# Zero-padding the 64-row contractions to 128 rows, with one relative-position row per head and queries in reverse order

## The chip, the core and the metric

The kernel runs on one core of a Trainium2 chip. The core has a matrix engine (PE; its weight loads, PEld, are listed apart), a vector engine (DVE), a scalar engine (ACT), GpSimd (POOL), and queues that start DMA transfers (SP's, ACT's, POOL's). The metric is the device time of one execution in microseconds (us), as a median over runs; lower is better.

## What is computed

Two transformer-like blocks of width 1024 run one after the other over the same 512 tokens, in float32. The parts that the change touches are these, cut to the core:

```python
# block 1, sliding-window attention: 8 heads of 64, 2 key heads, window 128
s = einsum("bnqkgd,bnskd->bnkgqs", qb, kb) * 64 ** -0.5      # contraction over 64
logits = where(valid, s + rel_table[rel_bucket(rel)], NEG_INF)   # bias by distance only
# block 1, indexed attention (DSA): 8 heads of 64 over a latent of 128
q_lat = einsum("bthd,hcd->bthc", q, w_uk) * 64 ** -0.5       # contraction over 64
dots  = einsum("bqhd,bsd->bqhs", iq, ik) * 64 ** -0.5        # 8 indexer heads of 64
score = einsum("bqh,bqhs->bqs", iw, relu(dots)); idx = top_k(score, 128)
logits = einsum("bqhc,bqkc->bhqk", q_lat, c_kv[idx]) + rel_table[rel_bucket(t - idx)]
# block 2, MLA: 16 heads, scores over 128 (nope) + 64 (rope) dimensions
q_full, k_full = concat([q_nope, q_rope]), concat([k_nope, k_rope])
s = einsum("bqhd,bkhd->bhqk", q_full, k_full) * 192 ** -0.5
```

Around them stand dense products: input and output projections, a cross attention to 256 memory rows, a feed-forward of 4096, and a state-space mixer (SSM) in block 2.

## The kernel before

Every float32 product is made of three matmuls on halves: a tensor is split in a high part H and a rest L, and `mm3` (L126 to L130) adds H·H, L·H and H·L in one PSUM bank. Weights arrive on SP's queue as `wraw` (512 KB, from `win_s` and the like); ACT rounds them to `wh` (L120), POOL subtracts for `wl` (L123). The framework gives each engine one in-order stream; a scheduler fixes the order when the program is built, and releases of tiles and PSUM banks become waits.

The program goes through these stages, in us of the span: memory keys, layer norm and the first input projections (0 to 90); the indexer (90 to 137), where PE also makes the memory values (`mem_v`, tile `acc`); more input projections with the top-k rounds on DVE (to 172); sliding-window attention, `swa`, with three more projections as filler (to 237); the DSA heads (to 300); the output projection, cross attention and feed-forward; the SSM mixer; MLA's input projection (to 1457), MLA's 16 heads (1457 to 1685) and the output projection.

Where the contraction is 64 long, the matmul uses 64 of PE's 128 rows:

- Indexer, per head and block of 128 queries: L446 multiplies all 128 rows (H of the query in one half, L in the other, both against `ikT` H), L447 multiplies the 64 rows of the H half by `ikT` L. ACT takes the relu (`rl`, L449), DVE adds it up (`sc`, L451 and L453). `ev_iq` (L407) fills `iq`; the L half goes to the other rows by a DMA on SP's queue (L414).
- `swa` scores: `sc<-kaH,qaH` and its two fellows, on the half that belongs to the key head.
- DSA `proj(h)` (L487): `mm<-qbH,wh`, 64 rows.
- MLA `scores`: three matmuls of 128 rows for nope, one of 128 rows for the rope part (L1371), one of 64 rows (L1372), for each of 16 heads and 4 blocks.

The bias by distance comes from a row per head. `bias_rows` (L820) makes these rows and writes each of them 64 times to DRAM, in `usd` (8 x 64 x 384) and `udd` (8 x 64 x 640). `bias_tile` (L816) reads a tile in which each partition starts one element earlier than the one above it, in two transfers of 64 rows: `bA` for `swa`, `bB` (one buffer) for DSA.

`attn_pipeline` (L870) runs a head's projection two heads ahead. The pool `dsaq`, which holds `bB` and `ql`, is opened before `swa`, so the scheduler can place work of the first DSA heads in `swa`'s tail.

Of the kernel before, what the change touches and what calls it, by code (L numbers as in the profile page):

```python
# [7 lines left out]
F32 = mybir.dt.float32  # L8
# [4 lines left out]
P = 128  # L13
# [3 lines left out]
NEG = -1e30  # L17
BR = 64
ALPHA = 2.0 ** 0.25
# [6 lines left out]
class Net:  # L26
# [51 lines left out]
    def consts(self):  # L78
        nc = self.nc
        self.ident = self.load(self.cp, "ident", [P, P])  # L80
        self.identr = self.cp.tile([P, P], F32R, tag="identr", name="identr")
        nc.vector.tensor_copy(self.identr, self.ident)
        self.mhalf = self.cp.tile([P, 16], F32, tag="mhalf", name="mhalf")
        nc.vector.memset(self.mhalf, -0.5)
        self.eps = {}
        for e in (1e-5, 1e-6):
            self.eps[e] = self.cp.tile([P, 1], F32, tag=f"eps{e}", name=self.nm("eps"))
            nc.vector.memset(self.eps[e], 4 * e)
        t = self.cp.tile([P, 1], F32, name="root")
        nc.scalar.activation(t, self.eps[1e-5], AF.Sqrt)  # L90
# [198 lines left out]
    def block1(self, dbg):  # L289
# [46 lines left out]
        dp = ctx.enter_context(self.tc.tile_pool(name="dp", bufs=1, space=bass.MemoryType.DRAM))  # L336
        usd = dp.tile([8, BR, 384], F32, name="usd")
        udd = dp.tile([8, BR, 640], F32, name="udd")
        ap = ctx.enter_context(self.pool("attn"))
# [11 lines left out]
        sq = c2.enter_context(self.pool("selfq"))  # L351
        ka = self.pair(sq, [P, T], "ka")
        qa = self.pair(sq, [P, 4, T], "qa")
        ikT = self.pair(sq, [P, T], "ikT")
        c3 = ExitStack()
        ap = c3.enter_context(self.pool("small"))
# [19 lines left out]
        ssq = ap.tile([P, NT], F32, name="ssq")  # L376
        junk = ap.tile([P, P], F32, name="junk")
        for v in vp:
# [3 lines left out]
        for t in range(NT):  # L382
            nc.vector.tensor_tensor(ms[t], accs[t][:, :328], bm, op=ALU.add)
            m = ms[t]
            nc.vector.tensor_scalar_mul(iw[:, t, :], m[:, 320:328], 8.0 ** -0.5)
            nc.scalar.activation(junk, m[:, 128:256], AF.Square, accum_out=ssq[:, t:t + 1])
# [20 lines left out]
        def ev_iq(i, ps):  # L407
            L = self.mp.tile([P, T], F32R, tag="vo", name=self.nm("ql"), bufs=2)
            for x, lo in zip(iq, (0, 64)):
                b = slice(lo, lo + 64)  # L410
                nc.scalar.activation(x[b, i, :], ps[b], AF.Identity, bias=bs[b, i:i + 1])
                nc.vector.scalar_tensor_tensor(L[b], ps[b], bs[b, i:i + 1], f32(x[b, i, :]), op0=ALU.add, op1=ALU.subtract)
            for x, lo in zip(iq, (0, 64)):
                nc.sync.dma_start(f32(x[64 - lo:128 - lo, i, :]), f32(L[lo:lo + 64]))  # L414

        def ev(i, ps):
            if i < 4:
                return ev_iq(i, ps)
            H, L = [None, ka, (x[:, i - 5, :] for x in qa), (x[:, i - 9, :] for x in qb)][0 if i < 4 else 1 if i < 5 else 2 if i < 9 else 3]
            if 4 <= i < 9:  # L420
                F = self.mp.tile([P, T], F32, tag="vo", name=self.nm("qf"), bufs=2)
                self.split_g(H, L, ps, F, bs[:, i:i + 1])
# [5 lines left out]
        for src, dst in ((ikf, ikT), (cf, cT)):  # L428
# [3 lines left out]
            self.split(dst[0], dst[1], ps)  # L432
        self.split(cM[0], cM[1], cf)
# [4 lines left out]
        for n in range(1, NT):  # L438
# [3 lines left out]
            for h in range(8):  # L442
                half = slice((h % 2) * 64, (h % 2) * 64 + 64)
                ps = self.mm()
                x = iq[h % 2]
                nc.tensor.matmul(ps[:, :w], x[:, h // 2, q], ikT[0][:, :w], start=True, stop=False, skip_group_check=True)  # L446
                nc.tensor.matmul(ps[:, :w], x[half, h // 2, q], ikT[1][half, :w], start=False, stop=True, skip_group_check=True)  # L447
                rl = self.mp.tile([P, 512], F32, tag="vo", name=self.nm("rl"), bufs=2)
# [22 lines left out]
        self.banks(sc=2, tr=2, pv=1, uv=1, mm=2)  # L471
        c4 = ExitStack()
        dq = c4.enter_context(self.pool("dsaq", "right"))
        mixA = self.pair(pa, [P, 4, T], "iq")
        self.swa(c2, mixA, qa, ka, vp, snk, usd, lambda x: self.gemm_s([a["win_s"][9 + x]], xt, lambda i, ps: ev(x + 9, ps)))
        self.flush()
        c2.close()
        sp = ctx.enter_context(self.pool("dsa"))
        self.gemm_s([a["win_s"][12]], xt, lambda i, ps: ev(12, ps))
# [3 lines left out]

        ukH, ukL = self.wload(a["w_uk"], n=512)
        uvH, uvL = self.wload(a["w_uv"])
        st = {}

        def proj(h):
            half = slice((h % 2) * 64, (h % 2) * 64 + 64)
            uc = slice((h // 2) * P, (h // 2 + 1) * P)  # L490
            bt = dq.tile([P, 512], F32, tag="bB", name=self.nm("bB"), bufs=1)
            self.bias_tile(bt, udd, h, 640, 512)
            ps = self.mm()
            self.mm3(ps, ukH[half, uc], ukL[half, uc], qb[0][half, h // 2, :], qb[1][half, h // 2, :], True, True)
            ql = self.pair(dq, [P, T], "ql", bufs=2)
# [8 lines left out]
        def out(h, PT):  # L504
# [8 lines left out]
            if h % 2 == 1:  # L513
                self.split(mix[0][:, 4 + h // 2, :], mix[1][:, 4 + h // 2, :], st["o"])
        self.attn_pipeline(sp, 8, proj, scores, out)
# [60 lines left out]
    def mem_k(self, W, wk):  # L576
        nc, a, mp = self.nc, self.a, self.mp

        def evk(i, ps):
            o = mp.tile([P, 256], F32, tag="ko", name=self.nm("ko"), bufs=3)  # L580
            nc.scalar.activation(o, ps, AF.Identity, bias=self.kb[:, i:i + 1])
            nc.sync.dma_start(self.kd[:, i * 256:(i + 1) * 256], o)
# [162 lines left out]
    def swa(self, c2, mix, qa, ka, vp, snk, usd, fill):  # L745
# [6 lines left out]
        def scores(pr, kv):  # L752
            h = pr + 4 * kv
            half = slice(kv * 64, kv * 64 + 64)
            bt = sp.tile([P, 256], F32, tag="bA", name=self.nm("bA"), bufs=2)
            self.bias_tile(bt, usd, h, 384, 256)
            Ss = []
            for n0 in (0, 2):
# [5 lines left out]
                for i in range(2):  # L764
# [4 lines left out]
                    o = ps[:, i * 256 + lo:i * 256 + 256]  # L769
                    self.mm3(o, qa[0][half, pr, q], qa[1][half, pr, q], ka[0][half, ks], ka[1][half, ks], i == 0, True)  # L770
                for i in range(2):
# [14 lines left out]
        for x, (pr, kv) in enumerate(heads):  # L786
# [18 lines left out]
            if kv == 1:  # L805
                self.split(mix[0][:, pr, :], mix[1][:, pr, :], acco)
            if x % 2 == 0 and x < 6:
# [410 lines left out]
    def block2b(self, dbg):  # L1218
# [4 lines left out]
        ckv = self.pair(lp, [P, 2, T], "ckv")  # L1223
        kr = self.pair(lp, [P, T], "kr")
        cs = self.load(lp, "rope_cs", [P, NT, 32])
        sn = self.load(lp, "rope_sn", [P, NT, 32])
        dmask = self.load(lp, "dmask", [P, T])
        zd = self.dram.tile([P, 16, T], F32, name="zd")
        with self.pool("mlain") as ip, self.pool("mlaz", "right") as zp:
# [39 lines left out]
            def trk():  # L1269
# [94 lines left out]
        def scores(h, n):  # L1364
# [76 lines left out]
def host(inp):  # L1441
# [152 lines left out]
```

## Time and profile before

| | |
|---|---|
| median of 3 runs | 1775.38 us (1775.02 to 1777.21) |
| the profiled execution | 1775.11 us |
| its span, first to last instruction | 1772.9 us |
| outside the span | 2.2 us |
| mean granted clock of PE | 0.985 |
| busy share: PE, PEld, DVE, ACT, POOL | 96%, 83%, 52%, 47%, 51% |

The profile is of one execution. "Busy" counts the modelled duration of matmuls, which overlap in the pipeline, so a PE that is busy all the time need not run at its peak: the distance from one matmul's start to the next one's start tells how fast it goes. A wait is given with the instruction that ended it. The granted clock is 1.00 at the higher of PE's two levels (2.4 GHz) and 0.50 at the lower (1.2 GHz).

### The profile page before, as it was taken

What the parts mean: (1) busy time and instruction counts of PE and PEld (TensorE: products, weight loads), DVE (VectorE), ACT (ScalarE), POOL (GpSimd) and SP (SyncE); (2) the same over time, 40 slices, a digit from 0 to 9 for tenths busy, and PEclk for the clock granted to TensorE, in tenths of its full rate; (3) what the DMA queues carried; (4) which work ended last, traced back from release to release, by engine and by line L of the source; (5) the groups of instructions that cost most, each with busy time, mean ns of one, the idle gap of its engine ahead of it and who ended that gap; (6) DMA issues with size and microseconds to landing.
All of it is one profiled execution on the core that took longest, in us unless ns stands there. A gap on an engine that the chain in (4) does not pass through costs nothing.

```text
span 1772.9 us, 27243 instructions
## 1 busy us (share of the span) xinstructions
PE 1699.5 (96%) x10203; PEld 1478.9 (83%) x10203; DVE 923.4 (52%) x1981; ACT 835.1 (47%) x1692; POOL 901.4 (51%) x825
## 2 busy tenths in 40 slices
PE   6979999899999999999999899998999999999998
PEld 6857779898988888887878788888999888888898
DVE  7448864634653004403778877788130325656522
ACT  4434664443343124313557677766333435555532
POOL 5726432452465445544558778776444534334341
PEclk8989999999999999999999999999999999999999
DMA  7654221532232222222332222332344331112341
GB/s 286 191 102 142 73 72 43 187 123 72 72 131 95 95 95 96 91 92 94 128 115 101 76 95 99 108 107 78 143 135 134 132 107 63 60 49 91 106 137 48
DMA packets 69444, 189.02 MB, mean 107 GB/s; under 512 B 10224, under 2 KB 17304, under 8 KB 69056
## 3 DMA queue, kind: packets, MB, share of 16 engines
q1 hardware_dynamic: 50128, 152.69, 25.2%
q10 hardware_dynamic: 18896, 32.50, 6.4%
q0 software_dynamic: 288, 2.10, 0.3%
q8 instruction: 80, 1.31, 0.3%
q14 instruction: 52, 0.43, 0.1%
HBM read 163.59 MB, written 16.84 MB: 102 GB/s over the span
## 4 chain that ended last, share of the span: by engine, by line
PE 74%; DVE 11%; ACT 5%; DMA 5%; issue 3%; POOL 2%; ACTq 0%; DVEq 0%; SPq 0%; POOLq 0%
PE mm L128 13%; PE mm L130 12%; PE mm L129 12%; PE acc L129 5%; PE acc L128 5%; PE acc L130 5%; PE sc L128 3%; PE sc L129 2%; PE sc L130 2%; DMA Dm<-acd 2%; DVE xbc L923 2%; PE pv L129 2%; PE pv L128 2%; PE pv L130 2%; PE tr L862 1%
## 5 line engine op out<-in xcount | busy, mean ns | idle before, releaser
L123 POOL TENSOR_TENSOR wl<-wraw,wh 128x512 fp32r<-128x512 f32 (+3 forms) x497 | 662.9, 1357 | 537.3 <-ACT wh L120 521.8
L120 ACT ACTIVATE wh<-wraw 128x1024 fp32r<-128x1024 f32 (+5 forms) x254 | 257.9, 1017 | 427.2 <-PE acc L130 125.5
L128 PE MATMUL mm<-xaH,wh 128*128 128x512 f32 x552 | 222.1, 402 | 0.0
L130 PE MATMUL mm<-xaH,wl 128*128 128x512 f32 x552 | 221.8, 402 | 0.0
L129 PE MATMUL mm<-xaL,wh 128*128 128x512 f32 x552 | 221.2, 401 | 0.0
L128 PE MATMUL mm<-wh,xaH 128*128 128x256 f32 x512 | 145.2, 284 | 1.4 <-ACT xaH L144 1.4
L130 PE MATMUL mm<-wh,xaL 128*128 128x256 f32 x512 | 144.6, 284 | 0.9 <-DVE xaL L142 0.9
L129 PE MATMUL mm<-wl,xaH 128*128 128x256 f32 x512 | 144.0, 282 | 0.0
L130 PEld LDWEIGHTS mm<-xaH,wl 128*128 128x128 f32 x552 | 105.3, 191 | 24.8
L128 PEld LDWEIGHTS mm<-xaH,wh 128*128 128x128 f32 x552 | 105.4, 191 | 24.4 <-issue 0.4
L129 PEld LDWEIGHTS mm<-xaL,wh 128*128 128x128 f32 x552 | 105.4, 191 | 24.3
L853 POOL TENSOR_SCALAR S<-S,den 128x128 f32<-128x128 f32 (+1 forms) x96 | 50.9, 533 | 122.1 <-DVE den L852 111.6
L128 PEld LDWEIGHTS mm<-wh,xaH 128*128 128x128 f32 x512 | 96.5, 188 | 2.0 <-ACT xaH L144 1.8
L130 PE MATMUL mm<-wh,xbL 128*128 128x256 f32 x336 | 94.7, 285 | 2.4 <-DVE xbL L142 2.3
L130 PEld LDWEIGHTS mm<-wh,xaL 128*128 128x128 f32 x512 | 96.0, 188 | 1.1 <-DVE xaL L142 1.1
L129 PEld LDWEIGHTS mm<-wl,xaH 128*128 128x128 f32 x512 | 96.5, 189 | 0.2
L128 PE MATMUL mm<-wh,xbH 128*128 128x256 f32 x336 | 95.2, 284 | 0.7 <-DVE lnsum L255 0.5
L129 PE MATMUL mm<-wl,xbH 128*128 128x256 f32 x336 | 94.5, 282 | 0.0
L680 DVE TENSOR_TENSOR rl<-rl 128x512 f32<-128x512 f32 x32 | 42.3, 1321 | 80.3 <-ACT rl L679 80.3
L923 DVE SCALAR_TENSOR_TENSOR xbc<-mm,conv_w,xbc 128x511 f32<-128x511 f32 (+2 forms) x84 | 62.2, 742 | 18.4 <-ACT xbc L921 17.5
L130 PEld LDWEIGHTS mm<-wh,xbL 128*128 128x128 f32 x336 | 62.8, 188 | 3.5 <-DVE xbL L142 2.9
L851 ACT ACTIVATE S<-S,mx 128x128 f32<-128x128 f32 (+1 forms) x96 | 53.7, 560 | 23.6 <-DVE mx L850 21.9
(616 smaller groups left out, 4777.9 us busy)
## 6 DMA issues: line engine op xcount, KB each, us to landing
wraw<-in_w_up SPq DMA_DIRECT2D x32, 512.0 KB, 3.2
wraw<-in_w_down SPq DMA_DIRECT2D x32, 512.0 KB, 3.2
wraw<-in_ssm_xbc SPq DMA_DIRECT2D x32, 512.0 KB, 3.2
Dm<-acd ACTq DMA_DIRECT2D x32, 256.0 KB, 3.4
wraw<-in_ssm_out SPq DMA_DIRECT2D x16, 512.0 KB, 3.5
wraw<-in_mla_z SPq DMA_DIRECT2D x16, 512.0 KB, 3.5
wraw<-in_mla_out SPq DMA_DIRECT2D x16, 512.0 KB, 3.5
wraw<-in_ssm_z SPq DMA_DIRECT2D x14, 512.0 KB, 3.3
```

The lines of the kernel that those rows point to most:

```text
L120: nc.scalar.activation(h[:, :n], raw[:, :n], AF.Copy)
L123: (leng or nc.gpsimd).tensor_tensor(l[:, e], raw[:, e], f32(h[:, e]), op=ALU.subtract)
L128: mm(out, aH, bH, start=first, stop=False, skip_group_check=True)
L129: mm(out, aH, bL, start=False, stop=False, skip_group_check=True)
L130: mm(out, aL, bH, start=False, stop=last, skip_group_check=True)
L680: nc.vector.tensor_tensor(r, r, r, op=ALU.mult)
L851: nc.scalar.activation(s, s, AF.Exp, bias=mx, scale=-1.0, accum_out=den)
L853: nc.gpsimd.tensor_scalar(s, s, den, 1.0, op0=ALU.mult, op1=ALU.mult)
L862: self.nc.tensor.transpose(pt[:, c], S[:, c], self.ident)
L923: nc.vector.scalar_tensor_tensor(o[:, j:], ps[:, :T - j], cw[:, m, 3 - j:4 - j], o[:, j:], op0=ALU.mult, op1=ALU.add)
```

## The change

All contractions of 64 get 128 rows, of which 64 are zero. `ka` becomes two pairs of tiles, one for each key head, with the other half zeroed; `ikT` L gets zeros in its upper half and H of every indexer query now stands in the lower half; `w_uk` is padded in DRAM (512 KB in place of 256 KB); MLA's `kr` H gets zeros in its lower half. The zeros are written by GpSimd.

The rows of relative positions are written once per head. A read then starts one element later on each next partition, and so the queries of a block stand in reverse order; `rev` turns them round when PSUM is read into `qa`, `qb` and, after attention, into the mix, and the identity for the masks (`identr`) is reversed too. The pool `dsaq` is opened after `swa`'s pool is closed. Two scratch tiles move to other memory.

```diff
-        nc.vector.tensor_copy(self.identr, self.ident)
+        b = self.identr[:, P - 1:P]
+        nc.vector.tensor_copy(bass.AP(b.tensor, b.offset, [b.ap[0], [-1, P]]), self.ident)
...
-        usd = dp.tile([8, BR, 384], F32, name="usd")
-        udd = dp.tile([8, BR, 640], F32, name="udd")
+        usd = dp.tile([8, 384], F32, name="usd")
+        udd = dp.tile([8, 640], F32, name="udd")
...
-        ka = self.pair(sq, [P, T], "ka")
+        ka = [self.pair(sq, [P, T], f"ka{kv}") for kv in range(2)]
+        for kv in range(2):
+            o = slice(64 - kv * 64, 128 - kv * 64)
+            for x in ka[kv]:
+                nc.gpsimd.memset(f32(x[o, :]), 0.0)
...
+        nc.gpsimd.memset(f32(ikT[1][64:, :]), 0.0)
...
+            if i == 4:
+                F = self.mp.tile([P, T], F32, tag="vo", name=self.nm("kf"), bufs=2)
+                for kv in range(2):
+                    b = slice(kv * 64, kv * 64 + 64)
+                    self.split_g(ka[kv][0][b, :], ka[kv][1][b, :], ps[b], F[b, :], bs[b, i:i + 1])
+                return
+            H, L = (self.blocks(x[:, i - 5, :] if i < 9 else x[:, i - 9, :]) for x in (qa if i < 9 else qb))
+            ps = self.rev(ps)
...
-                nc.tensor.matmul(ps[:, :w], x[half, h // 2, q], ikT[1][half, :w], start=False, stop=True, skip_group_check=True)
+                nc.tensor.matmul(ps[:, :w], x[:, h // 2, q], ikT[1][:, :w], start=False, stop=True, skip_group_check=True)
...
-        c4 = ExitStack()
-        dq = c4.enter_context(self.pool("dsaq", "right"))
         mixA = self.pair(pa, [P, 4, T], "iq")
         self.swa(c2, mixA, qa, ka, vp, snk, usd, lambda x: self.gemm_s([a["win_s"][9 + x]], xt, lambda i, ps: ev(x + 9, ps)))
         self.flush()
         c2.close()
+        c4 = ExitStack()
+        dq = c4.enter_context(self.pool("dsaq", "right"))
...
-            self.mm3(ps, ukH[half, uc], ukL[half, uc], qb[0][half, h // 2, :], qb[1][half, h // 2, :], True, True)
+            self.mm3(ps, ukH[:, uc], ukL[:, uc], qb[0][:, h // 2, :], qb[1][:, h // 2, :], True, True)
...
-                    self.mm3(o, qa[0][half, pr, q], qa[1][half, pr, q], ka[0][half, ks], ka[1][half, ks], i == 0, True)
+                    self.mm3(o, qa[0][:, pr, q], qa[1][:, pr, q], ka[kv][0][:, ks], ka[kv][1][:, ks], i == 0, True)
...
     def bias_tile(self, bt, ud, h, n, w):
-        for lo in range(0, P, BR):
-            self.nc.scalar.dma_start(bt[lo:lo + BR], bass.AP(ud.tensor, ud.offset + h * BR * n + 127 - lo, [[n - 1, BR], [1, w]]))
+        self.nc.scalar.dma_start(bt, bass.AP(ud.tensor, ud.offset + h * n, [[1, P], [1, w]]))
+    def rev(self, x):
+        b = x[:, P - 1:P]
+        return bass.AP(b.tensor, b.offset, [b.ap[0], [P, NT], [-1, P]])
+    def blocks(self, x):
+        return x.rearrange("p (n c) -> p n c", c=P)
...
-        nc.scalar.dma_start(usd, us.unsqueeze(1).to_broadcast([8, BR, 384]))
-        nc.scalar.dma_start(udd, ud.unsqueeze(1).to_broadcast([8, BR, 640]))
+        nc.scalar.dma_start(usd, us)
+        nc.scalar.dma_start(udd, ud)
...
+        nc.gpsimd.memset(f32(kr[0][0:64, :]), 0.0)
...
-                nc.tensor.matmul(ps[:, :w], qr[64:, q], kr[0][64:, :w], start=False, stop=True, skip_group_check=True)
+                nc.tensor.matmul(ps[:, :w], qr[:, q], kr[0][:, :w], start=False, stop=True, skip_group_check=True)
```

The change also moves instructions where `swa` goes over into the DSA heads. On ACT's queue before, in the tail of `swa` (`PTAH` and `iqH<-uv` are `swa`'s, `S`, `bB` and `qlH` those of the first DSA heads), the second head's `bB` is read ahead of `swa`'s last evacuation `iqH_1545<-uv_2196`:

```order
L851 ACTIVATE S_2385,den_2387<-S_2385,mx_2386 128x256 [waits DVE_49]
L144 ACTIVATE iqH_1545<-pv_2010 128x512 [waits PE_49]
L851 ACTIVATE S_2397,den_2399<-S_2397,mx_2398 128x384 [waits DVE_49]
L144 ACTIVATE PTAH_2197<-tr_2205 128x512 [waits PE_49]
L141 ACTIVATE qlH_2528<-mm_2524 128x512 [waits PE_49]
L144 ACTIVATE PTAH_2224<-tr_2226 128x384 [waits PE_49,Activation_49]
L851 ACTIVATE S_2409,den_2411<-S_2409,mx_2410 128x512 [waits DVE_49]
L818 DMA bB_2418<-udd 64x512 [waits DMAHW3_49]
L818 DMA bB_2418<-udd 64x512
L144 ACTIVATE PTAH_2224<-tr_2232 128x512 [waits PE_49]
L851 ACTIVATE S_2433,den_2435<-S_2433,mx_2434 128x128 [waits DVE_49]
L144 ACTIVATE iqH_1545<-uv_2196 128x512 [waits PE_49]
```

On ACT's queue of the change, at the same place:

```order
L145 ACTIVATE PTAH_2222<-tr_2224 128x384 [waits DVE_49,PE_49]
L145 ACTIVATE PTAH_2222<-tr_2230 128x512 [waits PE_49]
L145 ACTIVATE iqH_1551<-uv_2194 128x512 [waits PE_49]
L835 DMA bB_2360<-udd 128x512 [waits DVE_49]
L142 ACTIVATE qlH_2366<-mm_2362 128x512
L142 ACTIVATE qlH_2425<-mm_2421 128x512
L876 ACTIVATE S_2374,den_2376<-S_2374,mx_2375 128x128 [waits DVE_49]
```

The first DSA head's `bB` and the `qlH` of heads 0 and 1 now stand behind `swa`'s last evacuation, and `bB` waits for DVE. On PE before, the scores of DSA head 1 (`sc` from `cTH` and `qlH`) stand among `swa`'s last `uv` matmuls; those of head 0 came earlier still:

```order
L128 MATMUL sc_2429<-cTH_538,qlH_2425 128x128
L129 MATMUL sc_2429<-cTL_539,qlH_2425 128x128
L130 MATMUL sc_2429<-cTH_538,qlL_2426 128x128
L128 MATMUL uv_2196<-PTAH_2197,vpH_536 128x256
L837 MATMUL sc_2444<-mk_542,identr 128x256
L128 MATMUL sc_2444<-cTH_538,qlH_2425 128x256
L129 MATMUL sc_2444<-cTL_539,qlH_2425 128x256
L130 MATMUL sc_2444<-cTH_538,qlL_2426 128x256
L129 MATMUL uv_2196<-PTAL_2198,vpH_536 128x256
```

On PE of the change, `swa`'s last `uv` matmul comes first, then the scores of head 0:

```order
L131 MATMUL uv_2194<-PTAH_2222,vpL_537 128x128
L129 MATMUL sc_2370<-cTH_538,qlH_2366 128x128
L130 MATMUL sc_2370<-cTL_539,qlH_2366 128x128
L862 MATMUL sc_2381<-mk_542,identr 128x256
L129 MATMUL sc_2381<-cTH_538,qlH_2366 128x256
L130 MATMUL sc_2381<-cTL_539,qlH_2366 128x256
L131 MATMUL sc_2370<-cTH_538,qlL_2367 128x128
L131 MATMUL sc_2381<-cTH_538,qlL_2367 128x256
L129 MATMUL mm_2523<-qbH_532,wh_2347 128x512
```

All score matmuls of the DSA heads have moved behind `swa`; the projections of heads 0 and 1 stay inside it. In MLA and the rest, PE's order is essentially the old one.

## Rows read from the trace of the kernel before

**Rows 1.** The page: busy time, share of the span and instructions by engine.

```profile
PE 1699.5 (96%) x10203; PEld 1478.9 (83%) x10203; DVE 923.4 (52%) x1981; ACT 835.1 (47%) x1692; POOL 901.4 (51%) x825
```

**Rows 2.** Stretches: us, busy PE, PEld, DVE, ACT, POOL, granted clock, DMA share, GB/s.

```profile
90.00:100.00 10.00, 10.00 (x50) 7.69 (x49) 3.47 (x5) 3.97 (x6) 5.11 (x5) 1.00 0.60 90
100.00:110.00 10.00, 5.02 (x17) 2.96 (x15) 0.00 (x0) 0.00 (x0) 0.00 (x0) 0.84 0.65 124
110.00:120.00 10.00, 5.68 (x12) 3.31 (x12) 4.37 (x5) 3.75 (x8) 3.69 (x3) 0.50 0.54 110
120.00:130.00 10.00, 10.00 (x34) 5.97 (x33) 7.14 (x13) 4.06 (x9) 2.11 (x3) 0.98 0.61 105
130.00:140.00 10.00, 10.00 (x22) 5.37 (x22) 8.44 (x16) 4.54 (x8) 0.58 (x2) 0.71 0.31 82
```

**Rows 3.** Waits from 80 to 140 us: waiter, releaser, total us, times, longest.

```profile
ACT rl L449 <- DMA iqL<-ql: 15.8, 1, 15.8
```

**Rows 4.** DMA queues and issues from 80 to 140 us (KB each, landing).

```profile
q10 hardware_dynamic: 1040, 2.10, 30.8%
...
wraw<-in_win_s SPq DMA_DIRECT2D x4, 512.0 KB, 19.1
wraw<-in_xa_wv SPq DMA_DIRECT2D x3, 512.0 KB, 3.7
udd<-ng_dsa ACTq DMA_DIRECT2D x1, 1280.0 KB
usd<-ng_swa ACTq DMA_DIRECT2D x1, 768.0 KB
```

**Rows 5.** PE in order of time in the indexer: start, modelled duration.

```profile
131.36 0.50 PE L446 MATMUL mm<-ikTH,iqL 128*128 128x512 f32 x1
131.79 0.50 PE L447 MATMUL mm<-ikTL,iqL 64*128 64x512 f32 x1
```

**Rows 6.** PE in order of time in an MLA head.

```profile
1463.74 0.34 PE L130 MATMUL sc<-knH,qnL 128*128 128x384 f32 x1
1463.92 0.33 PE L1371 MATMUL sc<-krL,xbH 128*128 128x384 f32 x1
1464.18 0.44 PE L1372 MATMUL sc<-krH,xbH 64*128 64x384 f32 x1
1464.55 0.50 PE L128 MATMUL sc<-knH,qnH 128*128 128x512 f32 x1
1464.89 0.40 PE L129 MATMUL sc<-knL,qnH 128*128 128x512 f32 x1
1465.12 0.40 PE L130 MATMUL sc<-knH,qnL 128*128 128x512 f32 x1
```

**Rows 7.** Line L1372: idle before it and who waited for it (us, times).

```profile
  issue: 9.7, 32
...
  DVE S L850: 20.8, 21
```

**Rows 8.** Busy time in the MLA heads, 1460 to 1660 us, sum of five stretches.

```profile
sum 200.00, PE 198.24 PEld 161.78 DVE 119.60 ACT 112.90 POOL 80.82; mean PE 39.65 PEld 32.36 DVE 23.92 ACT 22.58 POOL 16.16
```

**Rows 9.** Busy time from 172 to 240 us, sum of seven stretches.

```profile
sum 68.00, PE 67.69 PEld 55.32 DVE 57.57 ACT 45.60 POOL 31.16; mean PE 9.67 PEld 7.90 DVE 8.22 ACT 6.51 POOL 4.45
```

**Rows 10.** PE in order of time, two 64-row matmuls on different halves.

```profile
96.09 0.38 PE L447 MATMUL mm<-ikTL,iqH 64*128 64x256 f32 x1
96.10 0.38 PE L447 MATMUL mm<-ikTL,iqL 64*128 64x256 f32 x1
```

**Rows 11.** PE in order of time: the last `uv` matmul of `swa`.

```profile
236.58 0.27 PE L130 MATMUL uv<-PTAH,vpL 128*128 128x128 f32 x1
```

**Rows 12.** Tile `bB`: its reader on DVE (ns min/median/max), and time to landing.

```profile
L850 DVE CUSTOM_DVE_ANT_0 S<-sc,bB x32: 282/480/692, 227.5 to 294.0; 128x128 f32<-128x128 f32 x8, 128x256 f32<-128x256 f32 x8, 128x384 f32<-128x384 f32 x8, 128x512 f32<-128x512 f32 x8
...
DMA to landing us min/median/max: 2.6/3.4/6.4
```

**Rows 13.** POOL's first real work in order of time.

```profile
9.48 2.37 POOL L145 TENSOR_TENSOR mtL<-mraw,mtH 128x1024 fp32r<-128x1024 f32 x1 [9.05 <-ACT mtH L144]
```

More of the change, by code (lines that the diff above doesn't have):

```diff
@@ L17 @@
 NEG = -1e30
-BR = 64
 ALPHA = 2.0 ** 0.25
@@ L303, in block1 @@
         xload = lambda t: nc.sync.dma_start(res[t], a["x"][t * P:(t + 1) * P, :])
+        self.kop = lnp
         memT = self.mem_load(mp, lnp)
@@ L376, in block1 @@
         ssq = ap.tile([P, NT], F32, name="ssq")
-        junk = ap.tile([P, P], F32, name="junk")
         for v in vp:
@@ L385, in block1 @@
             nc.vector.tensor_scalar_mul(iw[:, t, :], m[:, 320:328], 8.0 ** -0.5)
-            nc.scalar.activation(junk, m[:, 128:256], AF.Square, accum_out=ssq[:, t:t + 1])
+            nc.scalar.activation(cf[:, t, :], m[:, 128:256], AF.Square, accum_out=ssq[:, t:t + 1])
             nc.vector.bn_stats(st[:, t, :], m[:, 256:320])
@@ L407, in ev_iq @@
         def ev_iq(i, ps):
[L408 to L414, printed above, removed]
+            O = self.mp.tile([P, T], F32R, tag="vo", name=self.nm("qo"), bufs=2)
+            lo, hi = slice(0, 64), slice(64, P)
+            for b, H, L in ((lo, iq[0][lo, i, :], O[lo]), (hi, O[hi], iq[1][hi, i, :])):
+                nc.scalar.activation(H, ps[b], AF.Identity, bias=bs[b, i:i + 1])
+                nc.vector.scalar_tensor_tensor(L, ps[b], bs[b, i:i + 1], f32(H), op0=ALU.add, op1=ALU.subtract)
+            nc.sync.dma_start(f32(iq[0][hi, i, :]), f32(O[lo]))
+            nc.sync.dma_start(f32(iq[1][lo, i, :]), f32(O[hi]))
         def ev(i, ps):
@@ L418, in ev @@
                 return ev_iq(i, ps)
-            H, L = [None, ka, (x[:, i - 5, :] for x in qa), (x[:, i - 9, :] for x in qb)][0 if i < 4 else 1 if i < 5 else 2 if i < 9 else 3]
-            if 4 <= i < 9:
+            if i == 4:
[6 more added lines that the diff above has]
+            ps = self.rev(ps)
+            if i < 9:
                 F = self.mp.tile([P, T], F32, tag="vo", name=self.nm("qf"), bufs=2)
-                self.split_g(H, L, ps, F, bs[:, i:i + 1])
+                self.split_g(H, L, ps, self.blocks(F), bs[:, i:i + 1])
             else:
@@ L427, in block1 @@
         self.bias_rows(ap, rows, usd, udd)
-        for src, dst in ((ikf, ikT), (cf, cT)):
+        for src in (ikf, cf):
             ps = self.mm()
@@ L431, in block1 @@
                 nc.tensor.transpose(ps[:, t * P:(t + 1) * P], src[:, t, :], self.ident)
-            self.split(dst[0], dst[1], ps)
+            if src is cf:
+                self.split(cT[0], cT[1], ps)
+                continue
+            nc.scalar.activation(ikT[0], ps, AF.Copy)
+            nc.vector.tensor_tensor(ikT[1][0:64, :], ps[0:64], f32(ikT[0][0:64, :]), op=ALU.subtract)
         self.split(cM[0], cM[1], cf)
@@ L442, in block1 @@
             for h in range(8):
-                half = slice((h % 2) * 64, (h % 2) * 64 + 64)
                 ps = self.mm()
@@ L482, in block1 @@
             nc.gpsimd.dma_start(f32(x[:, 0:4, :]), f32(y))
-        ukH, ukL = self.wload(a["w_uk"], n=512)
+        ukH, ukL = self.wload(a["w_uk"])
         uvH, uvL = self.wload(a["w_uv"])
@@ L488, in proj @@
         def proj(h):
-            half = slice((h % 2) * 64, (h % 2) * 64 + 64)
-            uc = slice((h // 2) * P, (h // 2 + 1) * P)
+            uc = slice(h * P, (h + 1) * P)
             bt = dq.tile([P, 512], F32, tag="bB", name=self.nm("bB"), bufs=1)
@@ L513, in out @@
             if h % 2 == 1:
-                self.split(mix[0][:, 4 + h // 2, :], mix[1][:, 4 + h // 2, :], st["o"])
+                self.split(*[self.blocks(x[:, 4 + h // 2, :]) for x in mix], self.rev(st["o"]))
         self.attn_pipeline(sp, 8, proj, scores, out)
@@ L579, in evk @@
         def evk(i, ps):
-            o = mp.tile([P, 256], F32, tag="ko", name=self.nm("ko"), bufs=3)
+            o = self.kop.tile([P, 256], F32, tag="ko", name=self.nm("ko"), bufs=3)
             nc.scalar.activation(o, ps, AF.Identity, bias=self.kb[:, i:i + 1])
@@ L753, in scores @@
             h = pr + 4 * kv
-            half = slice(kv * 64, kv * 64 + 64)
             bt = sp.tile([P, 256], F32, tag="bA", name=self.nm("bA"), bufs=2)
@@ L805, in swa @@
             if kv == 1:
-                self.split(mix[0][:, pr, :], mix[1][:, pr, :], acco)
+                self.split(*[self.blocks(x[:, pr, :]) for x in mix], self.rev(acco))
             if x % 2 == 0 and x < 6:
@@ L1272, in trk @@
                     nc.tensor.transpose(ps[:, t * P:(t + 1) * P], krf[:, t, :], self.ident)
-                for x in kr:
-                    nc.scalar.activation(x, ps, AF.Copy)
+                nc.scalar.activation(kr[1], ps, AF.Copy)
+                nc.scalar.activation(kr[0][64:, :], ps[64:], AF.Copy)
                 nc.vector.tensor_tensor(kr[1][64:, :], ps[64:], f32(kr[1][64:, :]), op=ALU.subtract)
@@ L1480, in host @@
     uk = g("dsa_w_uk")[0]
-    o["w_uk"] = c(uk.transpose(0, 2, 1).reshape(4, P, P).transpose(1, 0, 2).reshape(P, 512))
+    pad = np.zeros((2, 64, 4, 2, P), np.float32)
+    for h in range(8):
+        pad[h % 2, :, h // 2, h % 2] = uk[h].T
+    o["w_uk"] = pad.reshape(P, 1024)
     uv = g("dsa_w_uv")[0]
```

## The prediction, made before the changed kernel ran

> **What bounds the kernel now.** I read the page first. PE is busy 96% of the span, the vector engine, ACT and POOL about half [rows 1]. So what shortens PE's stream, or removes one of the few stretches in which PE has nothing to do, shortens the kernel. The slices of the page point to one such stretch, and the busy time by stretch shows it: from 100 to 110 us DVE, ACT and POOL do nothing at all, PE lacks 5.0 us of its 10 there and 4.3 us of the next 10, and its granted clock falls to 0.50 [rows 2]. The waits name the cause: ACT's `rl`, the first consumer of the indexer's matmuls, sits 15.8 us until the DMA `iqL<-ql` lands [rows 3]. The DMA view of the same stretch says why a 128 KB transfer is late: the queue of ACT writes 2.10 MB in 1040 packets, nearly all of it the 64-fold copies `usd` and `udd`, and a weight tile that lands in 3.7 us elsewhere takes 19.1 [rows 4].
>
> The order of time on PE shows the second cost. Between matmuls with the same number of rows the starts are 0.18 us apart at 384 columns and 0.23 at 512. Around one 64-row matmul they are not [rows 6]: 0.26 from L1371 to L1372, 0.37 from L1372 to the next, 0.34 between that one and its 512-column successor. Over the usual distances this is 0.08 + 0.19 + 0.11 = 0.38 us for one excursion to 64 rows and back. In the indexer, where 128 and 64 rows alternate, each 512-column matmul takes 0.43 instead of 0.23 [rows 5], 0.40 for a pair: the same price. PE counts as busy in all of it, because durations are modelled.
>
> **MLA heads.** The change makes 64 L1372 matmuls 128 rows long. At 0.38 each that is 24 us; adding up start distances over all 64 places of the trace, less the usual distance of the same width, I get 23. Is it realised? PE is busy 198.24 of 200 us, and DVE, ACT and POOL 119.6, 112.9 and 80.8 [rows 8], so the others have room: shortened by 23 us, DVE would be at 68%. DVE's `S` waits 20.8 us in 21 places for the very L1372 matmul [rows 7], so its consumer is ready too. I take **-21.5**. The lower bound is the 9.7 us that PE's weight loads stand idle before these matmuls [rows 7]: **-10** if only this is saved and the rest turns into waits; the upper bound is -24. One memset for `kr` lies ahead of the heads, where POOL is no bound: nothing.
>
> **Indexer.** `usd` and `udd` shrink from 768 and 1280 KB to 12 and 20 KB, a 64th. With that traffic gone, `iqL` lands some 15 us sooner (a four times larger weight tile takes 3.7 us [rows 4]). What then sets the end, which is now at 137 us? PE would gain 9.3 us of idle time, some 3.6 us of work at the lower clock between 100 and 120 (half of 5.68, and 16% of 5.02) and about 2 near 135 where the clock is again 0.71, and 22 excursions at 0.40, 8.8: it could end 23.7 us sooner. DVE allows less: what it does from 110 to 140 is 19.95 us [rows 2], and put end to end behind 98 us it ends at 118, 19 us sooner. Two engines in step are never that tight. I take **-16.5**; bounds -11 (idle time and two thirds of the clock only) and -19.
>
> **Sliding window and the step to DSA.** The 64-row matmuls of `swa` stand in 19 runs between others, as I count them in PE's order of time: 19 x 0.38 = 7.2 us of PE. But DVE is busy 57.57 of 68 us there [rows 9], so I count -5 (bounds -7 and 0). The DSA projections give another -1.
>
> Against this, a new hole. `dsaq` is now opened after `swa` is closed, so the first `bB` waits for DVE's last evacuation, and in ACT's in-order queue `qlH` of heads 0 and 1 and all of their `S` stand behind it. The scores that filled PE before `swa`'s last matmul at 236.6 [rows 11] come after it. The work itself is only moved; the start-up of the DSA heads is what shows. Two evacuations of some 0.69 (the longest DVE operation of that size), 3.4 for `bB` to land, four L850 of 0.48 [rows 12], and an estimated 1.5 for the exponentials and the normalisation before the first transposes: 8.2 us. PE can lay into it the scores of two blocks and two projections, some 2.2 us. I take **+6**; bounds +2 (it slides in sooner) and +15 (the third rival).
>
> **Costed at nothing.** Five memsets of 64x512 go to the head of POOL's queue, which has no work until 9.48 us [rows 13]; without that cover they would cost about 0.6 us each, an estimate from a quarter of the 2.37 us of a POOL operation of 128x1024. Padded `w_uk` doubles a weight tile in a queue whose tiles land in 3.7 us. 16 bias reads replace 32 and free ACT's queue a little. No row shows a read of PSUM in reverse order; there are some 32 of these evacuations. From nothing to 0.69 us more each (a doubling): 0 to +22 on DVE and ACT together, and in `swa`, where DVE has 10 us to spare, at most some +5 on the end. As the element count is unchanged, I take 0.
>
> **A rule against the change.** A 64-row matmul uses half of PE's rows, and two on different halves can start 0.01 us apart [rows 10]. I found five such starts in the whole trace; the change gives up about 0.2 us at each, 1 us in all. The Trainium skill ("TensorE: Matmul & The Clock Gate", Why this matters for your kernels) says that a matmul over few rows takes as long as one over 128 and that the gain lies in running several row groups side by side. By that rule alone padding would save nothing and give up that overlap, and the sum would be that of the fourth rival; the trace agrees on the overlap, but shows it rarely.
>
> **Sum.** 1775.1 (the profiled execution, 0.3 us below the median) - 16.5 - 5 - 1 + 6 - 21.5 = **1737 us**. Its own range is 1728 to 1746.
>
> **Rivals.**
> 1. MLA passes to another bound: DVE or ACT chains take over after 10 us. Against it, the consumers wait for PE [rows 7]; for it, static orders leave gaps. 1748.5. Chance 0.11.
> 2. The indexer gives only -8: POOL's and DVE's chains, or weights that are still late, set the pace. For it: DVE at 8.44 of 10 in the last stretch [rows 2]. 1745.5. Chance 0.12.
> 3. The hole at DSA's start is +15: PE stands longer and its clock falls, as it did after the stall (0.50 for 10 us, [rows 2]). 1746. Chance 0.11.
> 4. The 0.38 us are not the price of changing row counts but of something that stays (the end of a PSUM group, other operands). Then MLA and `swa` give 0, the indexer -13 (stall and clock), and the hole +6: 1768. Against it: L130 to L1371 changes operands at 0.18 [rows 6], and the indexer shows the same price in another pattern. Chance 0.05.
> 5. Slower: the overlapping reads. All 128 rows of a `bB` now come from 2.5 KB of DRAM, and its tile has one buffer. Should landing grow from 3.4 us [rows 12], each of 8 heads waits the difference; it would eat the 38 us from a landing of 8.2 us on, and at 10 us gives 1737 + 8 x 6.6 = 1790. Nothing in the trace shows such a read, the size is unchanged. Chance 0.03.
>
> The forecast has 0.58. From 1726 (MLA and indexer near their upper bounds) to 1752 (one of the first three rivals, with some noise) lies about 0.8. Less than 0.2% (3.6 us) can't be told from no change: faster 0.95, same 0.02, slower 0.03.
>
> **What would show it.** In the profile after, `rl` no longer waits for `iqL`, DVE works through 100 to 110 us and the last `sc` ends near 120. In MLA, starts around L1372's successor are 0.17 to 0.23 us apart, and the stretch from the first to the last score is some 21 us shorter. PE shows idle time of about 6 us behind the last `uv` matmul. I am wrong if those start distances stay, if DVE's waits for PE in MLA are replaced by PE's for DVE or ACT, if `wraw<-in_win_s` still lands late, or if `bB` lands much later than 3.4 us.

## The result, and the profile after

The changed kernel takes 1730.9 us (median of 4 runs, 1726.7 to 1732.3) beside 1775.8 us for the kernel before: a ratio of 0.9742, 95% interval 0.9723 to 0.9762, so 44.9 us faster. The forecast was 1737 us; the time lies in its range, 6 us from its centre. The profiled execution took 1732.2 us, at the upper end of the four.

I matched the PE matmuls of both traces and read how far each has moved. Differences of that shift give the change by stage:

| stretch | forecast, us | profile, us |
|---|---|---|
| indexer and memory values, up to the projections behind | -16.5 | -22.9 |
| sliding window, its step to DSA, DSA heads | 0 (-5, -1, +6) | +0.1 |
| from there to MLA | 0 | +2.2 |
| MLA heads | -21.5 | -21.8 |
| all, on the span (1772.9 to 1730.5) | -38 | -42.4 |

About 2 us of the +2.2 are two stretches in which PE's clock is at its lower level (0.50). Busy time by stretch of the changed kernel, columns as in [rows 2]:

```profile
325.00:328.00 3.00, 3.00 (x16) 3.00 (x15) 2.93 (x5) 0.00 (x0) 2.88 (x2) 0.50 0.29 109
453.00:455.00 2.00, 2.00 (x11) 2.00 (x10) 1.96 (x4) 1.52 (x3) 2.00 (x2) 0.50 0.17 49
```

The kernel before has the lower level at the same two places, but for less time. Over 15 us around the first one (340 to 355 us before, 316 to 331 us after) the mean granted clock is 0.89 and 0.77, and it is 0.77 again in a second trace of the changed kernel (run 8). PE stands idle for 4.0 us just ahead of it in both kernels; why the lower level lasts longer after the change is open.

**The indexer.** The same view, 90 to 120 us; it answers to [rows 2]:

```profile
90.00:100.00 10.00, 10.00 (x54) 8.47 (x53) 4.29 (x7) 4.92 (x9) 5.37 (x5) 1.00 0.48 137
100.00:110.00 10.00, 10.00 (x51) 8.72 (x50) 8.71 (x12) 5.35 (x11) 5.86 (x5) 1.00 0.46 155
110.00:120.00 10.00, 9.34 (x39) 6.68 (x38) 8.87 (x16) 6.18 (x12) 0.57 (x1) 1.00 0.00 0
```

No engine stands still any more, the clock stays at 1.00, and from 100 us on DVE is the busiest engine beside PE. In the DMA view from 80 to 125 us, which answers to [rows 4], the copies are gone and weights land in 3.7 us in place of 19.1:

```profile
q10 hardware_dynamic: 32, 0.03, 0.5%
...
wraw<-in_win_s SPq DMA_DIRECT2D x4, 512.0 KB, 3.7
```

PE in order of time, which answers to [rows 5]: starts 0.23 to 0.24 us apart, where they were 0.43.

```profile
111.15 0.40 PE L465 MATMUL mm<-ikTH,iqL 128*128 128x512 f32 x1
111.39 0.39 PE L466 MATMUL mm<-ikTL,iqL 128*128 128x512 f32 x1
111.62 0.39 PE L465 MATMUL mm<-ikTH,iqH 128*128 128x512 f32 x1
```

**MLA.** The line of the former 64-row matmul (now L1398) has no idle time before it, and DVE waits for it 14.2 us in place of 20.8 [rows 7]. Its modelled duration has the median of L1397's (0.308):

```profile
L1398 PE MATMUL sc<-krH,xbH x32: 272/310/397, 1439.7 to 1602.2; 128*128 128x128 f32 x8, 128*128 128x256 f32 x8, 128*128 128x384 f32 x8, 128*128 128x512 f32 x8
...
its engine sat idle before it (us, times) until:
who waited for it (us, times):
  DVE S L875: 14.2, 20
```

PE is as full as in [rows 8], and DVE has risen from 60% to 67% of the stretch (1440 to 1625 us, sum of five):

```profile
sum 185.00, PE 183.05 PEld 165.22 DVE 124.69 ACT 114.97 POOL 83.38; mean PE 36.61 PEld 33.04 DVE 24.94 ACT 23.00 POOL 16.68
```

**The step to DSA.** PE in order of time behind `swa`'s last `uv` matmul; the bracket is idle time and what ended it:

```profile
207.04 0.27 PE L131 MATMUL uv<-PTAH,vpL 128*128 128x128 f32 x1
208.49 0.33 PE L129 MATMUL sc<-cTH,qlH 128*128 128x128 f32 x1 [1.18 <-ACT qlH L142]
...
210.35 0.63 PE L130 MATMUL mm<-qbL,wh 128*128 128x512 f32 x1
210.77 0.63 PE L131 MATMUL mm<-qbH,wl 128*128 128x512 f32 x1
211.20 0.63 PE L129 MATMUL mm<-qbH,wh 128*128 128x512 f32 x1
...
218.94 0.44 PE L862 MATMUL sc<-mk,identr 128*128 128x384 f32 x1 [1.05 <-DVE mx L875]
```

The hole is there: `qlH`, the operand named, stands behind `swa`'s evacuation in ACT's queue. PE's idle time behind that `uv` matmul is 2.6 us in four gaps up to 219 us, and not the 6 us that I had named as a sign. After the first gap the starts of 512-column matmuls are 0.43 apart for some 3 us where 0.23 is usual; the granted clock of 200 to 210 and 210 to 220 us is 0.94 and 0.89. One link of my chain is not there: the first `bB` does not wait for DVE's last evacuation (`iqL`), but goes out before it:

```profile
207.36 0.33 ACTq L835 DMA_DIRECT2D bB<-udd  x1
...
207.98 0.69 DVE L146 TENSOR_TENSOR iqL<-uv,iqH 128x512 fp32r<-128x512 f32 x1 [1.86 <-ACT iqH L145]
```

The tile view of `bB` (compare [rows 12]) shows that the read of overlapping rows takes no longer than 3.2 us:

```profile
DMA to landing us min/median/max: 3.0/3.0/3.2
```

### The profile page after: what moved, and what is told of

Read it like the earlier page. It is cut to its first block, busy times and chain, and to the rows that moved or that the text cites. A ratio compares the mean times of both kernels' runs of the same rounds, so it can differ in the third digit from the quotient of the medians.

```text
span 1730.5 us, 27236 instructions
## 1 busy us (share of the span) xinstructions
PE 1663.9 (96%) x10203; PEld 1479.8 (86%) x10203; DVE 927.3 (54%) x1981; ACT 834.1 (48%) x1694; POOL 907.9 (52%) x833
## 4 chain that ended last, share of the span: by engine, by line
PE 71%; DVE 14%; ACT 5%; issue 4%; DMA 3%; POOL 3%; ACTq 0%; DVEq 0%; SPq 0%; POOLq 0%
PE mm L129 12%; PE mm L131 12%; PE mm L130 12%; PE acc L129 5%; PE acc L130 5%; PE acc L131 5%; PE sc L130 2%; PE sc L131 2%; PE sc L129 2%; DMA Dm<-acd 2%; DVE xbc L948 2%; POOL wl L124 2%; PE pv L130 2%; PE pv L131 1%; PE pv L129 1%
## 5 line engine op out<-in xcount | busy, mean ns | idle before, releaser
L124 POOL TENSOR_TENSOR wl<-wraw,wh 128x512 fp32r<-128x512 f32 (+1 forms) x498 | 665.3, 1360 | 515.5 <-ACT wh L121 492.7
L121 ACT ACTIVATE wh<-wraw 128x1024 fp32r<-128x1024 f32 (+4 forms) x254 | 258.3, 1019 | 404.0 <-PE acc L131 123.7
L876 ACT ACTIVATE S<-S,mx 128x128 f32<-128x128 f32 (+1 forms) x96 | 53.7, 560 | 22.6 <-DVE mx L875 20.8
```

Of the source, the lines that this page charges most:

```text
L121: nc.scalar.activation(h[:, :n], raw[:, :n], AF.Copy)
L124: (leng or nc.gpsimd).tensor_tensor(l[:, e], raw[:, e], f32(h[:, e]), op=ALU.subtract)
L876: nc.scalar.activation(s, s, AF.Exp, bias=mx, scale=-1.0, accum_out=den)
```

## The experiments

Each run has a profile; ratios are to the kernel before on the same chip, with 95% intervals. The runs come from several chips, on which the kernel before took 1774.4 to 1776.4 us; a difference of two runs in us, where they are from different chips, is uncertain by up to 2 us. Shifts by stage come from the traces.

**1. The copies put back.** The changed kernel, with 64-fold rows again (read with a step of one row and one element, so that the queries stay reversed):

```diff
-        self.nc.scalar.dma_start(bt, bass.AP(ud.tensor, ud.offset + h * n, [[1, P], [1, w]]))
+        for lo in range(0, P, 64):
+            self.nc.scalar.dma_start(bt[lo:lo + 64], bass.AP(ud.tensor, ud.offset + h * 64 * n + lo, [[n + 1, 64], [1, w]]))
...
-        nc.scalar.dma_start(usd, us)
+        nc.scalar.dma_start(usd, us.unsqueeze(1).to_broadcast([8, 64, 384]))
...
```

> The changed kernel with one part undone: each row of relative positions is written 64 times again and read in two transfers of 64 rows (reversed order and padding stay). Theory A, the 2 MB of copies on ACT's queue hold up the indexer's query halves: the stall comes back, PE loses about 9 us of idle time and 5 us to the lower clock, so about 1745 us, and `rl` waits some 15 us for a DMA. Theory B, the gain of the indexer came from the row counts on PE: no more than 2 us slower than 1731 us.

Measured: 1749.0 us, 0.9851 (0.9837 to 0.9864), 18 us slower than the changed kernel. Busy time by stretch and the waits from 80 to 130 us of this run show the old stall with all matmuls at 128 rows:

```profile
100.00:110.00 10.00, 1.06 (x6) 0.74 (x4) 0.00 (x0) 0.11 (x1) 0.00 (x0) 0.76 0.67 116
...
ACT rl L468 <- DMA iqL<-qo: 13.2, 1, 13.2
```

Theory A holds. In the traces it loses 16.1 us to the changed kernel up to the projections behind the indexer (0.7 us ahead, then 15.4 us late); another 1.1 us come by `swa`'s last `uv` matmul and 1.6 behind it, where the clock is lower for longer (0.77 from 220 to 235 us; the changed kernel has 0.89 from 204 to 219).

**2 and 3. The indexer's matmuls at 64 rows; the sliding window's at 64 rows.** The changed kernel with one slice each:

```diff
-                nc.tensor.matmul(ps[:, :w], x[:, h // 2, q], ikT[1][:, :w], start=False, stop=True, skip_group_check=True)
+                nc.tensor.matmul(ps[:, :w], x[0:64, h // 2, q], ikT[1][0:64, :w], start=False, stop=True, skip_group_check=True)
```

> The changed kernel with the indexer's second matmul over 64 rows again (the half that holds the data). Theory A, PE sets the pace of this stage once the copies are gone: 24 excursions at 0.2 to 0.4 us, 5 to 9 us slower than the changed kernel, 1736 to 1740 us. Theory B, DVE sets it, as my prediction had it: within 2 us of 1731 us.

Measured: 1737.0 us, 0.9789 (0.9772 to 0.9806), 6 us slower; 7.2 us in the trace by the projections behind. Theory A. PE sets the end of this stage. ACT's wait for these matmuls from 80 to 130 us is 11.0 us, where the changed kernel (80 to 125 us, below it) has 2.5:

```profile
ACT rl L468 <- PE mm L466: 11.0, 14, 2.1
```

```profile
ACT rl L468 <- PE mm L466: 2.5, 3, 0.9
```

The starts around one 64-row matmul of this run are 0.26, 0.37 and 0.33 us apart at 384, 384 and 512 columns, as in [rows 6], though it uses the lower half of the rows and MLA's the upper one.

```diff
-                    self.mm3(o, qa[0][:, pr, q], qa[1][:, pr, q], ka[kv][0][:, ks], ka[kv][1][:, ks], i == 0, True)
+                    hf = slice(kv * 64, kv * 64 + 64)
+                    self.mm3(o, qa[0][hf, pr, q], qa[1][hf, pr, q], ka[kv][0][hf, ks], ka[kv][1][hf, ks], i == 0, True)
```

> The changed kernel with the score matmuls of the sliding window over 64 rows again. Theory A, as my prediction had it, PE pays 19 excursions at 0.36 us and DVE leaves little room: 5 us slower than the changed kernel, 1736 us. Theory B, DVE (busy 10 of 10 us for 50 us on end) sets the pace here: within 2 us of 1731 us.

Measured: 1733.5 us, 0.9770 (0.9756 to 0.9785), 2.6 us slower, between the theories. In the traces this run loses 4.3 us to the changed kernel up to `swa`'s last `uv` matmul, and 2.8 us are left by the end of the DSA heads. What comes back comes at the step to DSA: the gap of 1.18 us behind the last `uv` matmul is there too, but this run's clock stays at 1.00 from 200 to 230 us, and the starts of the projections with 512 columns are 0.24 us apart, where the changed kernel has 0.43:

```profile
213.25 0.40 PE L129 MATMUL mm<-qbH,wh 128*128 128x512 f32 x1
213.49 0.39 PE L130 MATMUL mm<-qbL,wh 128*128 128x512 f32 x1
```

So the sliding window itself is worth 4.3 of PE's 7.2 us. That DVE takes the rest fits its being busy 10 of 10 us from 150 to 180 us in the changed kernel, but no run took DVE's work away to show it.

**4. MLA alone.** The kernel before with only this (and the lower half of `kr` H zeroed):

```diff
-                nc.tensor.matmul(ps[:, :w], qr[64:, q], kr[0][64:, :w], start=False, stop=True, skip_group_check=True)
+                nc.tensor.matmul(ps[:, :w], qr[:, q], kr[0][:, :w], start=False, stop=True, skip_group_check=True)
```

> The kernel before with one part of the change alone: the last MLA score matmul over 128 rows, half of them zeros. Theory A, each of 64 excursions to 64 rows costs PE 0.36 us and PE sets MLA's pace: about 22 us faster than before, 1754 us, nothing else moves. Theory B, other engines take over after the 9.7 us that the weight loads stood idle: about 1766 us. Theory C, the price is not the row count: 1776 us.

Measured: 1754.3 us, 0.9881 (0.9867 to 0.9894), 20.7 us faster. In its trace PE is within 0.5 us of the kernel before until MLA begins, and 21.8 us ahead when it ends. Theory A.

**5. An excursion or a matmul?** Three 64-row matmuls in a run, in the place of the two of 128 rows:

```diff
-                nc.tensor.matmul(ps[:, :w], qr[:, q], kr[1][:, :w], start=False, stop=False, skip_group_check=True)
-                nc.tensor.matmul(ps[:, :w], qr[:, q], kr[0][:, :w], start=False, stop=True, skip_group_check=True)
+                nc.tensor.matmul(ps[:, :w], qr[64:, q], kr[1][64:, :w], start=False, stop=False, skip_group_check=True)
+                nc.tensor.matmul(ps[:, :w], qr[64:, q], kr[0][64:, :w], start=False, stop=False, skip_group_check=True)
+                nc.tensor.matmul(ps[:, :w], qr[64:, q], kr[1][64:, :w], start=False, stop=True, skip_group_check=True)
```

> The changed kernel with the two rope matmuls of each MLA score block replaced by three over the same upper 64 rows, one behind the other (the product of the lower half is left out and one of the upper half is made twice). Theory A, the price is paid for an excursion, a leave and a return, however many 64-row matmuls stand in it: 64 excursions cost 23 us again, and 64 more matmuls at 0.11 to 0.23 us cost 10: 33 us slower than the changed kernel, 1764 us. Theory B, every 64-row matmul pays it: 192 x 0.36 = 69 us and the 10, 1810 us. Theory C, the price is not the row count: only the 10, 1741 us.

Measured: 1766.6 us, 0.9949 (0.9932 to 0.9965), 35.7 us slower than the changed kernel. Theory A. The lines of this run show where the price is paid: the first matmul of the run (L1397) has a median of 0.412 us and its weight load (PEld) idle time before it, the middle one (L1398) lasts what a matmul of 128 rows does:

```profile
L1397 PE MATMUL sc<-krL,xbH x32: 322/412/497, 1437.4 to 1627.1; 64*128 64x128 f32 x8, 64*128 64x256 f32 x8, 64*128 64x384 f32 x8, 64*128 64x512 f32 x8
...
  issue: 9.4, 30
...
L1398 PE MATMUL sc<-krH,xbH x32: 268/306/394, 1437.5 to 1627.5; 64*128 64x128 f32 x8, 64*128 64x256 f32 x8, 64*128 64x384 f32 x8, 64*128 64x512 f32 x8
```

Durations are modelled, so the starts are the firmer evidence. Over the usual distances of the same width, the medians are 0.09 us more on the way in, 0.10 from the first to the second, 0.00 from the second to the third, 0.09 on the way out and 0.10 behind it: before rounding 0.39 us for the whole run of three.

**6 and 7. Fewer copies.** The kernel before with another count:

```diff
-BR = 64
+BR = 32
```

> The kernel before with 32 in place of 64 copies of each row, read in four transfers of 32 rows. Theory A, the stall goes with the bytes on ACT's queue (18 us for 2 MB, by the run with the copies back): about 9 us faster than before, 1766 us, and weights of `win_s` land in about 10 us; the 32 additional issues on ACT may take back 1 to 3. Theory B, any late write is enough to hold the query halves up: 1774 to 1778 us.

Measured: 1776.8 us, 1.0013 (1.0002 to 1.0023): nothing gained. Theory A as I put it falls. The waits from 80 to 140 us show the stall unchanged, while the weights do land sooner (12.6 us):

```profile
ACT rl L449 <- DMA iqL<-ql: 16.1, 1, 16.1
```

The packets of the trace suggest why: 64 copies are written from 89 to 134 us, 32 copies from 89 to 112, and the last packets of `iqL` move near 113 in both. If the transfer needs until 113 us beside copies, halving took away only the part of them that came after that. So with `BR = 16`:

> The kernel before with 16 copies of each row, read in eight transfers of 16 rows. With 32 copies the writes still ran until 111.9 us, about as long as the stall lasts. Theory A, the query halves are held up for as long as copies are being written: 16 copies end near 101 us, `rl` waits less than 6 us for its DMA in place of 16, and the projections ahead of the sliding window come 8 to 12 us sooner. Theory B, the wait has another cause on SP's queue: it stays at 16 us. The whole time says little here, since 96 additional issues of 0.3 to 0.6 us stand in ACT's queue: 1765 to 1790 us.

Measured, in a single execution: 1776.3 us. Copies end at 101.5 us, the last packets of `iqL` move at 103 us, and the wait is 0.7 us longer than theory A had it:

```profile
ACT rl L449 <- DMA iqL<-ql: 6.7, 1, 6.7
```

The projections behind come 9.2 us sooner. Theory A, with one correction from the 64 copies, which run on past the landing: in these three traces the transfer crawls beside the copies, and comes sooner only where they end before it is through. The 9 us are lost again by the end of the DSA heads, where the reads come in eight transfers each; that these issues are the reason was not tried apart.

**8. The pool of the DSA queries opened early.** The changed kernel with the old place of `dsaq`; room for it comes from `ikT`, which goes to a pool that ends sooner:

```diff
-        ikT = self.pair(sq, [P, T], "ikT")
+        ikT = self.pair(self.mp, [P, T], "ikT")
...
+        c4 = ExitStack()
+        dq = c4.enter_context(self.pool("dsaq", "right"))
         mixA = self.pair(pa, [P, 4, T], "iq")
...
-        c4 = ExitStack()
-        dq = c4.enter_context(self.pool("dsaq", "right"))
...
```

> The changed kernel with the pool of the DSA queries opened before the sliding-window attention again; to make room, the indexer's keys lie in the pool that ends before it. Theory A, the late pool leaves a hole of 6 to 7 us at the start of the DSA heads: about 1725 us, and PE does not wait behind the last `uv` matmul. Theory B, DVE is the bound of the sliding window (busy 10 of 10 us in three stretches), so the work taken in there lengthens it by as much: 1730 to 1732 us.

Measured: 1723.4 us, 0.9709 (0.9695 to 0.9722). Beside the changed kernel once more, on one chip:

> The changed kernel itself, on the same chip as the run with the early pool: 1729 to 1732 us.

> The run with the early pool again, beside the changed kernel. If the gap of 7 us is the hole at the DSA heads, whose part up to 290 us was 5 us in the trace, it is 4 to 7 us faster than the changed kernel, 1723 to 1727 us; if most of it was chance (clock dips elsewhere), less than 3 us.

Measured: 1731.2 (0.9742, 0.9729 to 0.9756) and 1724.7 us (0.9704, 0.9691 to 0.9718). The early pool is worth 6.5 us and beats both kernels; theory A. Busy time by stretch from 200 to 220 us, first of the changed kernel in this pair, then with the early pool:

```profile
200.00:210.00 10.00, 7.56 (x42) 6.19 (x41) 5.14 (x12) 3.92 (x10) 1.70 (x3) 0.85 0.30 110
210.00:220.00 10.00, 8.86 (x47) 7.19 (x46) 6.15 (x24) 5.97 (x19) 2.99 (x6) 0.98 0.42 155
```

```profile
200.00:210.00 10.00, 9.93 (x72) 9.00 (x71) 6.94 (x26) 6.93 (x22) 4.10 (x9) 1.00 0.12 27
210.00:220.00 10.00, 8.24 (x46) 6.35 (x46) 6.01 (x20) 5.39 (x15) 3.19 (x6) 1.00 0.66 238
```

PE's 2.4 us of idle time in the first stretch are gone and its clock is not taken down there; 1.8 us of idle time are in the second. Not all of the 6.5 us is the hole: in the traces of this pair the early pool is 3.8 us ahead by the end of the DSA heads (5.0 in its first trace against the changed kernel's), and gains 2.0 more at the two places behind where the changed kernel's clock is at its lower level for longer (mean clock over 15 us there 0.77, with the early pool 0.89). Nor is the clock at the step safe: in the first trace of the early pool it falls a little later (0.84 from 220 to 230 us).

**9. A second buffer for `bB`**, on top of the early pool:

```diff
-            bt = dq.tile([P, 512], F32, tag="bB", name=self.nm("bB"), bufs=1)
+            bt = (sp if h % 2 else dq).tile([P, 512], F32, tag="bB", name=self.nm("bB"), bufs=1)
```

> The run with the early DSA pool, and `bB` of odd heads in a second buffer (in the DSA pool). There DVE waited 7.7 us for `bB` in 7 places, and PE stood 1.4 us for it at head 1. Theory A, one of these waits at the start is on the path: 1 to 3 us faster than that run's 1723.4 us. Theory B, PE has other work at all of them: 1722 to 1725 us.

Measured: 1726.7 us, 0.9731 (0.9716 to 0.9746). Theory A falls: DVE's waits for `bB` fall from 7.7 to 1.6 us, and nothing is gained. The run is 3.3 us slower than the first run of the early pool and 2.0 slower than the second, each on another chip, and the intervals of the ratios overlap; that it is slower at all is not shown. The scheduler also put the work of the DSA heads in another order. By 350 us its trace is level with the first early pool's again (0.4 us apart, as it was ahead of the DSA heads).

**10. The rows alone.** The changed kernel with all 64-row matmuls back, by the slices above and a like one in the DSA projections:

> The changed kernel with all 64-row matmuls back (indexer, sliding window, DSA projections, MLA): what is left is the single row per head, the reversed order and the late pool. Theory A, the parts add up: 1731 and 6 (indexer), 2.6 (sliding window), 21 (MLA) and about 1 (projections) make 1761 us. Theory B, they overlap, since the stages share DVE's top-k rounds: 1755 us or less.

Measured: 1765.3 us, 0.9947 (0.9930 to 0.9964), with a spread of 8 us between its runs. It agrees with adding up (theory A) better than with overlap. In its trace, against the changed kernel's, the parts are 7.2 us up to the projections behind the indexer, 4.4 from there to the end of the DSA heads, and 21.8 in MLA.

## Why the prediction was right

**MLA, right in mechanism and size.** 23 us on PE, -21.5 expected, -21.8 in the trace, in the change and alone. DVE and ACT had the room that [rows 8] showed; the wait of DVE shrank and none of PE's took its place, so rival 1 falls. Run 5 says what the 0.38 us are: the price of leaving the 128-row form and coming back, once for a run of 64-row matmuls, not once for each. Rival 4 falls. The rule that I weighed there (the Trainium skill, "TensorE: Matmul & The Clock Gate", Why this matters for your kernels) says that a matmul over few rows takes as long as one over 128. The middle matmul of run 5 agrees with it (median 0.306 us, beside 0.308 at 128 rows); the excursion, which decides here, is not in it.

**Indexer, cause right, what sets its end wrong.** The cause by [rows 3] and [rows 4] holds: the stall comes back with the copies. The step that failed is "DVE allows less": I let DVE's last `sc` set the end, and took -16.5. That `sc` did move by about what I said (137.4 to 119.7 us, the last of six in the line below; -17.7). But PE's next projections, which use `xaH`, don't wait for it. They start 4 us ahead of it, after 0.66 us for an earlier `rl`. PE in order of time and DVE in order of time, first before, then changed:

```profile
136.66 0.79 PE L128 MATMUL mm<-xaH,wh 128*128 128x512 f32 x1
...
137.40 0.75 DVE L453 SCALAR_TENSOR_TENSOR sc<-rl,iw,sc 128x512 f32<-128x512 f32 x1 [0.69 <-ACT rl L449]
```

```profile
115.69 0.51 PE L129 MATMUL mm<-xaH,wh 128*128 128x512 f32 x1 [0.66 <-ACT rl L468]
...
115.39 5.02 DVE L472 SCALAR_TENSOR_TENSOR sc<-rl,iw,sc 128x512 f32<-128x512 f32 x6
```

PE's own sum in that paragraph, 23.7 us, is what came: -22.9. DVE made up its lag afterwards in gaps it had before: its last top-k replacement moved from 200.0 to 177.5 us, by 22.5. Rival 2 falls. In the traces up to the projections, 16.1 us are the copies (run 1) and 7.2 the row counts (run 2).

**Sliding window, nearly right in itself.** I counted 5 of PE's 7.2 us; the trace of run 3 says 4.3 by its last matmul. Run 3's whole time says only 2.6, because 1.5 us come back at the step behind, where the clock falls in the changed kernel and not in run 3; the sum had no term for that.

**The hole, right in kind, its size in part by luck.** +6 expected, and 6.5 by the whole times of the pair of run 8, but 3.8 to 5.0 by the traces up to the end of the DSA heads; the rest of the 6.5 is mostly clock further behind. `qlH` stands behind ACT's evacuation as forecast, but `bB` does not wait for DVE's, and PE's idle time is 2.6 us and not 6. Rival 3's mechanism appears at a fraction of its price: the clock falls for some 3 us after the gap, which costs about 1.2 us against run 3, where it does not fall after the same gap.

**Costed at nothing, right.** An evacuation that reads PSUM in reverse order takes what it took: on ACT the line of `qaH` has a median of 0.680 us in the changed kernel, as before (0.67), and on DVE the `iqL` that reads `uv` takes 0.69 us in both. The memsets end at 3.3 us, before POOL's first work at 9.6. Rival 5 falls by the landing of 3.0 us.

Against the forecast of -38 the profile has -6.4 in the indexer, -0.3 in MLA, +0.1 in the sliding window and DSA and +2.2 between DSA and MLA, mostly clock: -42.4. The time came under the forecast mainly because of the indexer. The +0.1 adds up from the runs: -4.4 for the row counts of the sliding window and the DSA projections together (run 10) and +3.8 to +5.0 for the late pool (run 8). I had -6 and +6, both too large, so that the two errors cancel.

## What to carry to other kernels

Look at the distance of matmul starts, not at busy time: PE was "busy" through all of the 23 us that MLA gave back. Where contractions of different length alternate, group them or pad them with zeros; the price is one per excursion. When an off-path engine bounds a stage on paper, ask whether anything on the path really waits for its last result. And bulk writes with time to spare should not be issued just ahead of a small transfer that an engine waits for: halving them gained nothing as long as they were still running when that transfer passed.

## What was not expected of the hardware

The copies on ACT's queue slow transfers on SP's queue without a simple relation to their volume: ACT waits 15.8 us with 2 MB, 16.1 with 1 MB and 6.7 with 0.5 MB. What the two queues share was not tried. A read of 128 overlapping rows out of 2.5 KB of DRAM lands in 3.0 us, about as soon as its two halves of 64 rows from a copy in 1.3 MB, one issued after the other (median 3.4 us each before, 2.7 in run 1). And the same gap in PE's work is followed by the lower clock in one run and not in another: 1.18 us behind `swa`'s last `uv` matmul, with the clock of the next 3 us at 0.50 in the changed kernel and at 1.00 in run 3.
